# A two-layer decoder trunk: the list of each engine's work is made with the two DMA queues described packet by packet

## The chip, the cores and the metric

One core of one Trainium2 chip. The metric is device time in microseconds (us) of one execution, the median of several. Five engines run their own instruction streams and wait for each other by semaphores: PE (TensorE, matmuls; its weight loads are shown apart as PEld), DVE (VectorE), ACT (ScalarE), POOL (GpSimd) and SP (SyncE, which here only issues transfers). Transfers run in two queues over the same 16 DMA engines: those that SP (and once ACT) issues, called HW below, and those that POOL issues, called SW.

## The reference, cut to what matters

256 tokens of width 1024 in float32 go through two layers, each with a feed-forward part ahead of its attention and one behind it; the feed-forward width is 2816.

```
def swiglu(x, w_in, w_out):
    gate, up = jnp.split(x @ w_in, 2, axis=-1)
    return (jax.nn.silu(gate) * up) @ w_out

for layer in range(DEPTH):                       # DEPTH = 2
    h = h + 0.5 * swiglu(rms_norm(h, ffn1_norm[layer]), ffn1_w_in[layer], ffn1_w_out[layer])
    hn = rms_norm(h, mix_norm[layer])
    if layer < 1:
        q, k, v = heads(hn @ sb_w_qkv[layer])
        h = h + stick_breaking_attention(q, k, v) @ sb_w_o[layer]
    else:
        q = rotary(hn @ swa_w_q[0])
        h = h + sliding_window_sink_attention(q, k_shared, v_shared, sinks) @ swa_w_o[0]
    h = h + 0.5 * swiglu(rms_norm(h, ffn2_norm[layer]), ffn2_w_in[layer], ffn2_w_out[layer])
    if layer == 0:
        k_shared, v_shared = split(rms_norm(h, kv_norm) @ kv_w)
return rms_norm(h, final_norm)
```

## The kernel before, in words

**Stages.** The program runs, one after the other, FFN1 of layer 0 (the first feed-forward stage), stick-breaking attention, FFN2 of layer 0 (the second), the shared keys and values with FFN1 of layer 1 (the third), sliding-window attention, FFN2 of layer 1 (the fourth), and the last norm.

**Numbers.** A float32 product is made of three matmuls of 512 columns (one *step*): weights and activations are each split in a high part and the rest, and hi·hi, hi·lo and lo·hi are added up in PSUM. So each weight tile (1 MB, `raw`) is loaded by SP (`dma`, L369), cast on ACT to `w_hi` (L419), and DVE subtracts to get `w_lo` (L421), each in two halves of 1024 columns. All matmuls of weights have line L288.

**A feed-forward stage.** The first product (gate and up) is done in column blocks. Most blocks use a scheme with seven products in place of eight (`strassen`). Its four weight tiles r11, r12, r22 and r21 are loaded on SP. DVE forms r11 += r12 and later r11 += r22 (L611, two halves each). Two more sums are not made by DVE but by a *fetch* (L616): POOL issues a transfer that adds a block of weights from memory onto the tile, once onto r12 and once onto r11. Each fetch must wait until the earlier content of its tile has been cast, that is for a certain half of `w_lo` on DVE; the product with the tile follows when the fetch has landed and ACT and DVE have cast it. The last product of each stage's first part is the one on the r11 of the last block, after its second fetch. Meanwhile PE does the second product (the *out* weights, `w_out`, two rows of 128 a tile) of earlier blocks, its steps with `aT_h` and `aT_l` as moving operands.

There are five `raw` buffers. A load is issued on SP when the buffer's earlier content has been cast, so that a `w_lo` on DVE also releases SP's next load. `aT_l` (L498), `p`, `u`, `s`, `m` (L786, L789) are DVE's other work: the lower parts of transposed activations and the gating.

**What sets the order.** The code does not issue instructions directly. It makes tasks (`T`), each with an engine, a planned duration, what it reads and writes, and a priority. `Plan.order` lists them: `listed` simulates the five engines as servers that take, among their ready tasks, the one of highest priority; `due` goes back from the end and gives each task of the other engines the time at which PE must have it; with these as new priorities it lists again, four times, and the list with the shortest planned end is emitted. So durations in the plan decide the order of instructions on each engine. In the plan of before a load is a task on SP that lasts its bytes over a fixed rate, and the next load begins when it ends; 2000 ns more pass until its readers may start. A fetch is a task of 1500 on POOL and, in the same row on SP, an empty one that lasts its bytes over 170 (`ADDING`). Loads and fetches thus stand in one row, one at a time.

Of the kernel before, what the change touches and what calls it, by code (L numbers as in the profile page):

```python
# [17 lines left out]
P = 128  # L18
# [62 lines left out]
HEAD = 700.0  # L81
PASSES = 4
# [5 lines left out]
class Task:  # L88
    __slots__ = ("eng", "dur", "fn", "prio", "deps", "outs", "left", "ready", "start", "end", "seq", "lat")

    def __init__(self, eng, dur, fn, prio, seq, lat):
        self.lat = lat
# [23 lines left out]
class Plan:  # L116
# [3 lines left out]
    def add(self, eng, dur, fn, r=(), w=(), prio=None, lat=None):  # L120
# [19 lines left out]
        t.deps.discard(t)  # L140
        self.tasks.append(t)
        return t

    def lag(self, t, o):
        return t.lat if t.lat is not None else 0.0 if o.eng == t.eng and t.eng != "SP" else LAT[t.eng]

    def listed(self, prio):
        free = {e: HEAD for e in LAT}
        wait = {e: [] for e in LAT}
        queue = {e: [] for e in LAT}  # L150
        for t in self.tasks:
            t.ready, t.left = 0.0, len(t.deps)
            if t.left == 0:
                heapq.heappush(wait[t.eng], (t.ready, t.seq, t))
        done = []
        while True:
            best = None
            for e in LAT:
                if queue[e]:
                    at = free[e]  # L160
                elif wait[e]:
                    at = max(free[e], wait[e][0][0])
                else:
                    continue
                if best is None or at < best[0]:
                    best = (at, e)
            if best is None:
                break
            at, e = best
            while wait[e] and wait[e][0][0] <= at:  # L170
                t = heapq.heappop(wait[e])[2]
                heapq.heappush(queue[e], (prio[t.seq], t.seq, t))
            t = heapq.heappop(queue[e])[2]
            t.start = at
            free[e] = at + t.dur
            t.end = at + t.dur
            done.append(t)
            for o in t.outs:
                o.ready = max(o.ready, t.end + self.lag(t, o))
                o.left -= 1  # L180
                if o.left == 0:
                    heapq.heappush(wait[o.eng], (o.ready, o.seq, o))
        assert len(done) == len(self.tasks)
        return done, max(t.end for t in done)

    def due(self, done):
# [5 lines left out]
        for t in sorted(done, key=lambda t: (-t.start, -t.seq)):  # L192
            due[t.seq] = min([last.get(t.seq, 1e18)] + [due[o.seq] - self.lag(t, o) - t.dur for o in t.outs])
# [34 lines left out]
def kernel(  # L228
# [139 lines left out]
    def dma(src, dst, nbytes, w, prio, r=()):  # L368
        T("SP", nbytes / (283.0 if prio < -8.5e5 + 50 else 375.0 if prio < -8e5 else PLAIN), lambda: nc.sync.dma_start(out=dst(), in_=src), r=r, w=w, prio=prio)  # L369
# [245 lines left out]
    def fetch(dst, src):  # L615
        T("POOL", 1500, lambda: nc.gpsimd.dma_start(out=dst.ap, in_=src, accum_op=ALU.add), w=[(dst, 0), (dst, 1)],  # L616
          prio=plan.pos - LOADS, lat=500.0)
        T("SP", P * 2048 * 4 / ADDING, lambda: None, w=[(dst, 0), (dst, 1)], prio=plan.pos - LOADS)
# [895 lines left out]
    def last(t, pair):  # L1514
# [44 lines left out]
        for j, c, ks in ((0, slice(0, 320), (0,)), (1, cuts[1], (640,)), (0, slice(320, 640), (0, 512))):  # L1559
# [8 lines left out]
            T(by, 500, lambda j=j, c=c, now=now, q=nc.scalar if by == "ACT" else nc.sync: q.dma_start(out=out[0, ts(t), c], in_=hg[j].ap[:, now]),  # L1568
              r=[(hg[j], ("to", c.start))], prio=1e9)
# [42 lines left out]
```

## Time and profile before

| | |
|---|---|
| median of three runs | 923.02 us (922.31 to 923.92) |
| the profiled execution | 924.5 us, of it the profile's span 922.7 us |
| mean granted clock of PE | 0.997 |
| matmuls | 4420 |
| bytes moved | 214.43 MB, mean 232 GB/s |

How to read it: a group's line has the source line, the engine, the operation, what it writes and reads, a count, its busy time, the mean in ns, and the idle time just before with what ended it. In the waits, "PEld ps L288 <- DVE w_lo L421" means that the weight load of a matmul waited for DVE's w_lo; total, number and longest follow. In a timeline, a row has the start, the length, the instruction with its count, and in brackets the idle time ahead of it. In the table by stretches each engine's busy time is followed by its count, and the three numbers at the end are the granted clock of PE (1.00 is full), the DMA engines' busy share and GB/s. In the DMA view the last number is the time from issue to landing.

### The profile page before, as it was taken

Reading aid. Unit: us, or ns where it says so; the run is one execution under the profiler, and the core shown is the slowest. Engines: PE = TensorE matmul, PEld = TensorE weight load, DVE = VectorE, ACT = ScalarE, POOL = GpSimd, SP = SyncE. Lnnn points to the kernel's source line nnn. Section 1 sums busy time; section 2 is a strip of 40 time slices with the busy share of each in tenths; the row PEclk is TensorE's granted clock in tenths of the full one; section 3 lists DMA queues with packets and bytes.
Section 4 is the critical chain, followed back from the end, with each engine's and each line's share of the span. In section 5 each row is a group of like instructions: output and inputs, shape, how many; then the busy total and the mean of one; then the engine's idle time right before and its main releaser. Section 6 shows DMA issues by size and latency. Waiting matters only on the chain.

```text
span 922.7 us, 11848 instructions
## 1 busy us (share of the span) xinstructions
PE 905.2 (98%) x4420; PEld 739.5 (80%) x4420; DVE 816.6 (89%) x989; ACT 646.3 (70%) x935; POOL 66.8 (7%) x71
## 2 busy tenths in 40 slices
PE   9999999999999999999999999999999999999997
PEld 6888888788888877778788887887897787787776
DVE  8989898787967999898889999987789799999887
ACT  7867566777987865685588667755868676668563
POOL 2001010000000101010001001100000010001000
PEclk9999999999999999999999999999999999999999
DMA  9897999896752699989795999999843269998981
GB/s 336 302 255 191 299 300 244 260 267 190 242 183 92 138 272 273 242 261 258 206 337 156 246 255 260 288 280 244 305 151 115 92 146 259 303 230 250 302 220 46
DMA packets 107305, 214.43 MB, mean 232 GB/s; under 512 B 6256, under 2 KB 27760, under 8 KB 107248
## 3 DMA queue, kind: packets, MB, share of 16 engines
q1 hardware_dynamic: 85184, 170.49, 52.7%
q0 software_dynamic: 21648, 42.99, 27.1%
q8 instruction: 34, 0.56, 0.2%
q10 hardware_dynamic: 416, 0.20, 0.1%
q14 instruction: 23, 0.19, 0.1%
HBM read 212.62 MB, written 1.05 MB: 232 GB/s over the span
## 4 chain that ended last, share of the span: by engine, by line
PE 41%; DVE 24%; DMA 19%; issue 10%; ACT 6%; POOL 0%; ACTq 0%; POOLq 0%; DVEq 0%; SPq 0%
PE ps L288 38%; DMA raw<-in_ffn_w_in_dram 18%; DVE w_lo L421 15%; ACT w_hi L419 5%; DVE raw L611 4%; PE ps L491 1%; DVE aT_l L498 1%; PE ps L677 1%; PE ps L1346 1%; DMA raw<-in_ffn_w_out_dram 1%; DVE s L587 0%; DVE S_l L581 0%; DVE u L786 0%; DVE xT L498 0%; DVE p L786 0%
## 5 line engine op out<-in xcount | busy, mean ns | idle before, releaser
L421 DVE TENSOR_TENSOR w_lo<-raw,w_hi 128x1024 fp32r<-128x1024 f32 x424 | 498.3, 1217 | 52.9 <-ACT w_hi L419 51.7
L419 ACT CAST w_hi<-raw 128x1024 fp32r<-128x1024 f32 x424 | 424.4, 1050 | 141.5 <-DMA raw<-in_ffn_w_in_dram 69.8
L288 PE MATMUL ps<-w_hi,xT 128*128 128x512 f32 (+1 forms) x788 | 231.6, 378 | 1.9 <-ACT w_hi L419 1.8
L288 PEld LDWEIGHTS ps<-w_hi,xT 128*128 128x128 f32 x788 | 143.0, 190 | 28.9 <-ACT w_hi L419 2.9
L288 PE MATMUL ps<-w_lo,xT 128*128 128x512 f32 (+1 forms) x394 | 148.4, 377 | 2.1 <-DVE w_lo L421 2.0
L288 PE MATMUL ps<-w_hi,aT_h 128*128 128x512 f32 x354 | 140.0, 396 | 0.0
L288 PE MATMUL ps<-w_lo,aT_h 128*128 128x512 f32 x354 | 137.7, 389 | 0.0
L288 PE MATMUL ps<-w_hi,aT_l 128*128 128x512 f32 x354 | 137.4, 388 | 0.0
L288 PE MATMUL ps<-w_lo,S_h 128*128 128x512 f32 x320 | 126.1, 394 | 1.4 <-DVE w_lo L421 1.3
L288 PE MATMUL ps<-w_hi,S_h 128*128 128x512 f32 x320 | 126.2, 394 | 0.1
L288 PE MATMUL ps<-w_hi,S_l 128*128 128x512 f32 x320 | 124.7, 390 | 0.0
L611 DVE TENSOR_TENSOR raw<-raw 128x1024 f32<-128x1024 f32 x78 | 93.7, 1218 | 1.0 <-DMA raw<-in_ffn_w_in_dram 0.8
L288 PEld LDWEIGHTS ps<-w_lo,xT 128*128 128x128 f32 x394 | 74.5, 189 | 18.4 <-DVE w_lo L421 5.1
L616 POOL DMA_DIRECT2D raw<-in_ffn_w_in_dram x38 | 48.1, 1266 | 517.6 <-ACT w_hi L419 209.2
L288 PEld LDWEIGHTS ps<-w_lo,aT_h 128*128 128x128 f32 x354 | 66.5, 188 | 14.1
L288 PEld LDWEIGHTS ps<-w_hi,aT_l 128*128 128x128 f32 x354 | 66.6, 188 | 12.9
L288 PEld LDWEIGHTS ps<-w_hi,aT_h 128*128 128x128 f32 x354 | 66.5, 188 | 12.8
L288 PEld LDWEIGHTS ps<-w_lo,S_h 128*128 128x128 f32 x320 | 60.0, 188 | 18.6 <-DVE w_lo L421 6.2
L288 PEld LDWEIGHTS ps<-w_hi,S_h 128*128 128x128 f32 x320 | 60.1, 188 | 12.2 <-ACT u L782 0.5
L288 PEld LDWEIGHTS ps<-w_hi,S_l 128*128 128x128 f32 x320 | 60.1, 188 | 12.1
L497 ACT CAST aT_h<-ps 128x512 fp32r<-128x512 f32 (+1 forms) x48 | 26.3, 547 | 56.1 <-PE ps L677 56.1
L288 PE MATMUL ps<-xT,w_hi 128*128 128x512 f32 (+1 forms) x136 | 47.0, 395 | 0.0
(184 smaller groups left out, 942.3 us busy)
## 6 DMA issues: line engine op xcount, KB each, us to landing
raw<-in_ffn_w_in_dram SPq DMA_DIRECT2D x76, 1024.0 KB, 8.7
raw<-in_ffn_w_out_dram SPq DMA_DIRECT2D x44, 1024.0 KB, 6.4
raw<-in_ffn_w_in_dram POOLq DMA_DIRECT2D x38, 1024.0 KB, 9.3
raw<-in_sb_w_qkv_dram SPq DMA_DIRECT2D x12, 1024.0 KB, 8.8
raw<-in_ffn_w_in_dram SPq DMA_DIRECT2D x16, 512.0 KB, 6.6
raw<-in_ffn_w_in_dram SPq DMA_DIRECT2D x16, 256.0 KB, 5.5
raw<-in_sb_w_o_dram SPq DMA_DIRECT2D x4, 1024.0 KB, 5.7
raw<-in_swa_w_q_dram SPq DMA_DIRECT2D x4, 1024.0 KB, 9.1
```

The lines of the kernel that those rows point to most:

```text
L288: PE.matmul(ps, lhsT=lhsT, rhs=rhs, start=start, stop=stop, skip_group_check=True)
L419: T("ACT", act(m), lambda sl=sl: ACT.copy(out=flat(hi)[:, sl], in_=flat(raw)[:, sl]), r=[(raw, i) for i in rs] + first, w=[(hi, i) for i i ...
L421: T("DVE", dve(m), lambda sl=sl: DVE.tensor_sub(out=flat(lo)[:, sl], in0=flat(raw)[:, sl], in1=flat(hi)[:, sl].bitcast(F32)), r=[(raw, i) ...
L491: PE.matmul(bank.ap[:, i * P:(i + 1) * P], lhsT=s, rhs=ident, start=i == 0, stop=True, is_transpose=True, skip_group_check=True)
L497: T("ACT", act(n), lambda: ACT.copy(out=hi[2](), in_=src()), r=B(bank), w=[hi[0:2]])
L498: T("DVE", dve(n), lambda: DVE.tensor_sub(out=lo[2](), in0=src(), in1=hi[2]().bitcast(F32)), r=B(bank) + [hi[0:2]], w=[lo[0:2]])
L611: T("DVE", dve(m), lambda sl=sl: DVE.tensor_add(out=flat(dst)[:, sl], in0=flat(dst)[:, sl], in1=flat(src)[:, sl]), r=[(src, k) for k in ks ...
L616: T("POOL", 1500, lambda: nc.gpsimd.dma_start(out=dst.ap, in_=src, accum_op=ALU.add), w=[(dst, 0), (dst, 1)], prio=plan.pos - LOADS, lat=5 ...
L677: PE.transpose(out=tr.ap[:, i * P:(i + 1) * P], in_=m.ap[:, i * P:(i + 1) * P], identity=ident)
L1346: PE.matmul(z[par].ap[:, i_ * P:(i_ + 1) * P], lhsT=e.ap[:, par * 384 + c:par * 384 + c + P], rhs=ident, start=i_ == 0, stop=True, is_tran ...
```

## The change

`Plan.listed` becomes a simulation by events. A task may carry `moves`: a queue (HW or SW), a number of packets for each DMA engine and the ns of one. Issuing costs its engine 500 (SP) or 1000 (POOL); after a set-up time the transfer joins its queue; the two queues' heads share the DMA engines in turn, a packet of each; after the last packet and a landing time the task has ended. `due` takes a task's whole time from start to end. Nothing else of the program is edited: the tasks, what they read and write and their given priorities stay, and so does the work on every engine.

```
+RAMP = 500.0
+SETUP = {"HW": 1200.0, "SW": 1700.0}
+LANDS = {"HW": 900.0, "SW": 500.0}
+ISSUE = 500.0
+PACKET = {4096: 157.0, 2048: 84.0, 1024: 50.0}
+ADDED = 176.0
...
     def lag(self, t, o):
-        return t.lat if t.lat is not None else 0.0 if o.eng == t.eng and t.eng != "SP" else LAT[t.eng]
+        return 0.0 if t.moves else t.lat if t.lat is not None else 0.0 if o.eng == t.eng else LAT[t.eng]
...
+        def begin(e, now):
+            if ready[e] and free[e] <= now:
+                t = heapq.heappop(ready[e])[2]
+                t.start = now
+                free[e] = now + t.dur
+                done.append(t)
+                at(free[e], "free", t)
+                if t.moves:
+                    at(now + SETUP[t.moves[0]], "moves", t)
+                else:
+                    at(free[e], "end", t)
...
+        while events or queues["HW"] or queues["SW"]:
+            heads = {k: q[0] for k, q in queues.items() if q}
+            total = sum(h[2] for h in heads.values())
+            next_ = [(last + h[1] * total / h[2], k) for k, h in heads.items()]
+            over = min(next_) if next_ else (1e18, None)
+            now = min(over[0], events[0][0] if events else 1e18)
+            for h in heads.values():
+                h[1] -= (now - last) * h[2] / total
+            last = now
+            if over[0] <= now:
+                t = queues[over[1]].popleft()[0]
+                at(now + LANDS[over[1]], "end", t)
+                continue
+            while events and events[0][0] <= now:
+                _, _, what, t = heapq.heappop(events)
+                if what == "moves":
+                    k, n, each = t.moves
+                    queues[k].append([t, n * each + (0.0 if heads else RAMP), each])
+                elif what == "end":
+                    ended(t, now)
+                elif what == "ready":
+                    heapq.heappush(ready[t.eng], (prio[t.seq], t.seq, t))
             for e in LAT:
...
-            due[t.seq] = min([last.get(t.seq, 1e18)] + [due[o.seq] - self.lag(t, o) - t.dur for o in t.outs])
+            due[t.seq] = min([last.get(t.seq, 1e18)] + [due[o.seq] - self.lag(t, o) - (t.end - t.start) for o in t.outs])
...
     def dma(src, dst, nbytes, w, prio, r=()):
-        T("SP", nbytes / (283.0 if prio < -8.5e5 + 50 else 375.0 if prio < -8e5 else PLAIN), lambda: nc.sync.dma_start(out=dst(), in_=src), r=r, w=w, prio=prio)
+        size = max(p for p in PACKET if p == 1024 or p <= 4 * src.shape[-1])
+        T("SP", ISSUE, lambda: nc.sync.dma_start(out=dst(), in_=src), r=r, w=w, prio=prio, moves=("HW", nbytes / size / 16, PACKET[size]))
...
     def fetch(dst, src):
-        T("POOL", 1500, lambda: nc.gpsimd.dma_start(out=dst.ap, in_=src, accum_op=ALU.add), w=[(dst, 0), (dst, 1)],
-          prio=plan.pos - LOADS, lat=500.0)
-        T("SP", P * 2048 * 4 / ADDING, lambda: None, w=[(dst, 0), (dst, 1)], prio=plan.pos - LOADS)
+        T("POOL", 1000, lambda: nc.gpsimd.dma_start(out=dst.ap, in_=src, accum_op=ALU.add), w=[(dst, 0), (dst, 1)],
+          prio=plan.pos - LOADS, moves=("SW", P * 2048 * 4 / 2048 / 16, ADDED))
```

The source lines behind the edit move down by 28 to 30: w_lo is L421 before and L451 after, the sum L611 and L641, the fetch L616 and L646, SP's loads L369 and L399, the matmul L288 and L317.

Three places show what becomes of the order. Numbers behind a name count buffers and are not the same before and after. The first is DVE near the end of the third feed-forward stage, around the `w_lo` that releases the stage's last fetch. Before, raw_4872 is r11, onto which the fetch adds, and raw_4936 is the tile of the other product:

```order
L611 TENSOR_TENSOR raw_4872<-raw_4872,raw_4936 128x1024
L421 TENSOR_TENSOR w_lo_5008<-raw_4872,w_hi_4996 128x1024
L421 TENSOR_TENSOR w_lo_5017<-raw_4936,w_hi_4981 128x1024
L421 TENSOR_TENSOR w_lo_5008<-raw_4872,w_hi_4996 128x1024
L421 TENSOR_TENSOR w_lo_5017<-raw_4936,w_hi_4981 128x1024
L421 TENSOR_TENSOR w_lo_5044<-raw_4962,w_hi_5022 128x1024 x2
L421 TENSOR_TENSOR w_lo_5059<-raw_4894,w_hi_5049 128x1024 x2
```

and of the change, where raw_4803 is r11, raw_4841 the other tile, and raw_4909 the out weights' tile (raw_4962 before):

```order
L451 TENSOR_TENSOR w_lo_4990<-raw_4803,w_hi_4958 128x1024 x2
L451 TENSOR_TENSOR w_lo_5013<-raw_4841,w_hi_4971 128x1024 x2
L451 TENSOR_TENSOR w_lo_5029<-raw_4825,w_hi_5006 128x1024 x2
L451 TENSOR_TENSOR w_lo_5051<-raw_4909,w_hi_5036 128x1024
L528 TENSOR_TENSOR aT_l_4883<-ps_66,aT_h_4876 128x4x128
L451 TENSOR_TENSOR w_lo_5051<-raw_4909,w_hi_5036 128x1024
```

Before, the two products' halves alternate, so that r11 is free after the third `w_lo` and the other tile after the fourth; in the change r11 is free after the second and the other tile two later, and the r12 product's `w_lo` (raw_4825) come ahead of the out weights'.

The second place is PE a little later, at the stage's last product. Before, its weights are w_hi_5118 and w_lo_5128; w_hi_5022 and w_hi_5140 are out weights:

```order
L288 MATMUL ps_66<-w_hi_5022,aT_h_4867 128x512
L288 MATMUL ps_66<-w_hi_5022,aT_l_4878 128x512
L288 MATMUL ps_66<-w_lo_5044,aT_h_4867 128x512
L288 MATMUL ps_66<-w_hi_5118,xT_163 128x512 x2
L288 MATMUL ps_66<-w_lo_5128,xT_163 128x512
...
L288 MATMUL ps_66<-w_hi_5140,aT_h_5113 128x512
L288 MATMUL ps_66<-w_hi_5140,aT_l_5120 128x512
L288 MATMUL ps_66<-w_lo_5149,aT_h_5113 128x512
```

and of the change, where they are w_hi_5121 and w_lo_5134, and w_hi_5103 is the out weight of raw_5034, whose `w_lo` DVE has ahead of the last product's:

```order
L317 MATMUL ps_66<-w_hi_5103,aT_h_5108 128x512
L317 MATMUL ps_66<-w_hi_5103,aT_l_5119 128x512
L317 MATMUL ps_66<-w_lo_5113,aT_h_5108 128x512
L317 MATMUL ps_66<-w_hi_5121,xT_176 128x512 x2
L317 MATMUL ps_66<-w_lo_5134,xT_176 128x512
...
L317 MATMUL ps_66<-w_hi_5103,aT_h_5108 128x512
L317 MATMUL ps_66<-w_hi_5103,aT_l_5119 128x512
L317 MATMUL ps_66<-w_lo_5113,aT_h_5108 128x512
```

Steps of the out weights that stood ahead of the last product stand behind it: two here, six in the second stage, three in the fourth, one in the first.

The third place is SP at the program's start, before:

```order
L369 DMA hN_63<-in_x_dram 128x512 x2
L369 DMA raw_113<-in_ffn1_w_in_dram 128x512 x4
L369 DMA hN_63<-in_x_dram 128x512 x2
L369 DMA raw_185<-in_ffn1_w_in_dram 128x512 x4
L369 DMA raw_214<-in_ffn1_w_in_dram 128x512 x4
```

and of the change:

```order
L399 DMA hN_63<-in_x_dram 128x512 x2
L399 DMA raw_100<-in_ffn1_w_in_dram 128x512 x2
L399 DMA hN_63<-in_x_dram 128x512
L399 DMA raw_100<-in_ffn1_w_in_dram 128x512
L399 DMA hN_63<-in_x_dram 128x512
L399 DMA raw_100<-in_ffn1_w_in_dram 128x512
```

The second half of x (two tiles of `hN`) goes between the four parts of the first weight tile instead of behind them.

More of the change, by code (lines that the diff above doesn't have):

```diff
@@ L81 @@
 HEAD = 700.0
+RAMP = 500.0
[4 more added lines that the diff above has]
+ADDED = 176.0
 PASSES = 4
 class Task:
-    __slots__ = ("eng", "dur", "fn", "prio", "deps", "outs", "left", "ready", "start", "end", "seq", "lat")
+    __slots__ = ("eng", "dur", "fn", "prio", "deps", "outs", "left", "ready", "start", "end", "seq", "lat", "moves")
     def __init__(self, eng, dur, fn, prio, seq, lat):
-        self.lat = lat
+        self.lat, self.moves = lat, None
         self.eng, self.dur, self.fn, self.prio, self.seq = eng, dur, fn, prio, seq
@@ L118, in __init__, with add @@
         self.tasks, self.pos = [], 0.0
-    def add(self, eng, dur, fn, r=(), w=(), prio=None, lat=None):
+    def add(self, eng, dur, fn, r=(), w=(), prio=None, lat=None, moves=None):
         t = Task(eng, dur, fn, self.pos if prio is None else prio, len(self.tasks), lat)
@@ L140, in add @@
         t.deps.discard(t)
+        t.moves = moves
         self.tasks.append(t)
@@ L144, in lag, with at, ended @@
     def lag(self, t, o):
-        return t.lat if t.lat is not None else 0.0 if o.eng == t.eng and t.eng != "SP" else LAT[t.eng]
+        return 0.0 if t.moves else t.lat if t.lat is not None else 0.0 if o.eng == t.eng else LAT[t.eng]
     def listed(self, prio):
         free = {e: HEAD for e in LAT}
-        wait = {e: [] for e in LAT}
-        queue = {e: [] for e in LAT}
+        ready = {e: [] for e in LAT}
+        events, made = [], [0]
+        queues, last, done = {"HW": deque(), "SW": deque()}, 0.0, []
+        def at(time, what, t):
+            made[0] += 1
+            heapq.heappush(events, (time, made[0], what, t))
+        def begin(e, now):
[9 more added lines that the diff above has]
+                    at(free[e], "end", t)
+        def ended(t, now):
+            t.end = now
+            for o in t.outs:
+                o.ready = max(o.ready, now + self.lag(t, o))
+                o.left -= 1
+                if o.left == 0:
+                    at(max(o.ready, HEAD), "ready", o)
         for t in self.tasks:
@@ L153, in listed @@
             if t.left == 0:
[L154 to L157, printed above, removed]
-            for e in LAT:
[L159 to L182, printed above, removed]
+                at(HEAD, "ready", t)
+        while events or queues["HW"] or queues["SW"]:
[20 more added lines that the diff above has]
+                    heapq.heappush(ready[t.eng], (prio[t.seq], t.seq, t))
+            for e in LAT:
+                begin(e, now)
         assert len(done) == len(self.tasks)
@@ L1567, in last @@
             by = "ACT" if t == j == 1 else "SP"
-            T(by, 500, lambda j=j, c=c, now=now, q=nc.scalar if by == "ACT" else nc.sync: q.dma_start(out=out[0, ts(t), c], in_=hg[j].ap[:, now]),
-              r=[(hg[j], ("to", c.start))], prio=1e9)
+            T(by, ISSUE, lambda j=j, c=c, now=now, q=nc.scalar if by == "ACT" else nc.sync: q.dma_start(out=out[0, ts(t), c], in_=hg[j].ap[:, now]),
+              r=[(hg[j], ("to", c.start))], prio=1e9, moves=("HW", 8, PACKET[1024]))
     ffn(ffn2_w_in[1], ffn2_w_out[1], (A0, (4, 3) if NEWACC else A1), ((2, 5) if NEWACC else A2) + A3, last, ending=True, blocks=BL[3], roots=roots4)
```

## The prediction

> **What bounds the kernel now.** First the page: busy shares, then the costliest groups.
>
> ```profile
> PE 905.2 (98%) x4420; PEld 739.5 (80%) x4420; DVE 816.6 (89%) x989; ACT 646.3 (70%) x935; POOL 66.8 (7%) x71
> L421 DVE TENSOR_TENSOR w_lo<-raw,w_hi 128x1024 fp32r<-128x1024 f32 x424 | 498.3, 1217 | 52.9 <-ACT w_hi L419 51.7
> ```
>
> TensorE is occupied all but through, and the change leaves it the same 4420 matmuls. So the whole prize is time in which PE waits or runs slowly. The waits of the weight loads, which show the waits that the pipelined matmuls hide, are these four lines:
>
> ```profile
> PEld ps L288 <- DVE w_lo L421: 11.3, 19, 1.0
> PEld ps L677 <- DVE m L789: 4.8, 5, 1.5
> PEld ps L288 <- ACT w_hi L419: 3.6, 5, 1.7
> PEld ps L677 <- DVE aT_l L498: 3.2, 7, 0.8
> ```
>
> Together 22.9 us. That, and what a slowed clock costs, is the most that any order of the same work can win. The largest single place is the end of the third feed-forward stage (FFN1 of layer 1), in the timeline of PE and in the table by stretches:
>
> ```profile
> 643.64 0.39 PE L288 MATMUL ps<-w_hi,aT_l 128*128 128x512 f32 x1
> 643.86 0.39 PE L288 MATMUL ps<-w_lo,aT_h 128*128 128x512 f32 x1
> 645.50 0.73 PE L288 MATMUL ps<-w_hi,xT 128*128 128x512 f32 x2 [1.25 <-ACT w_hi L419]
> 646.76 0.77 PE L288 MATMUL ps<-w_lo,xT 128*128 128x512 f32 x1 [0.53 <-DVE w_lo L421]
> 647.33 1.06 PE L288 MATMUL ps<-w_hi,xT 128*128 128x512 f32 x2
> ...
> 645.10:650.00 4.90, 3.98 (x10) 2.90 (x11) 4.52 (x4) 3.18 (x4) 0.00 (x0) 0.67 0.16 45
> ```
>
> Normal pace is 643.86 − 643.64 = 0.22 us, call it 0.227, a matmul. After idle times of 1.25 and 0.53 us two matmuls take 1.06 − 0.39 + 0.23 ≈ 0.86 us instead of 0.45 (the granted clock is 0.67 in the stretch). Some eight or nine matmuls at 0.2 us extra make 1.8 us, so the place costs 1.25 + 0.53 + 1.8 and small change, 3.9 us. The Trainium skill (TensorE: Matmul & The Clock Gate, "Part 1: The HAM clock gate (the "warmup" mystery)") has the clock halved only after an idle window of about 3.4 us; by that rule there would be no 1.8 us here. The row goes against it, and the row decides: a stall under 2 us can cost as much again.
>
> What PE waits for there is the last fetch (an accumulating transfer of 1 MB that POOL issues), then the cast on ACT, then w_lo on DVE. The chain that ended last shows the last fetch of each of the four stages, and what follows one of them:
>
> ```profile
> 147.41 12.89 DMA raw<-in_ffn_w_in_dram
> ...
> 442.67 12.99 DMA raw<-in_ffn_w_in_dram
> ...
> 455.68 1.06 ACT w_hi L419
> ...
> 456.76 1.24 DVE w_lo L421
> ...
> 597.80 12.70 DMA raw<-in_ffn_w_in_dram
> 629.93 14.44 DMA raw<-in_ffn_w_in_dram
> ...
> 883.59 13.83 DMA raw<-in_ffn_w_in_dram
> ```
>
> Fetches are not always that long. These are two others, from the DMA view of 505 to 516 us and of 566 to 578 us:
>
> ```profile
> raw<-in_ffn_w_in_dram POOLq DMA_DIRECT2D x1, 1024.0 KB, 8.7
> ...
> raw<-in_ffn_w_in_dram POOLq DMA_DIRECT2D x1, 1024.0 KB, 10.2
> ```
>
> And this is when POOL issued them, beside the next load that SP issued:
>
> ```profile
> 505.74 1.27 POOL L616 DMA_DIRECT2D raw<-in_ffn_w_in_dram  x1 [10.58 <-DVE w_lo L421]
> ...
> 566.52 1.27 POOL L616 DMA_DIRECT2D raw<-in_ffn_w_in_dram  x1 [8.48 <-DVE w_lo L421]
> ...
> 509.64 8.17 SPq L369 DMA_DIRECT2D raw<-in_ffn_w_in_dram  x3
> ...
> 568.47 9.71 SPq L369 DMA_DIRECT2D raw<-in_ffn_w_in_dram  x4
> ...
> 598.64 9.67 SPq L369 DMA_DIRECT2D raw<-in_ffn_w_in_dram  x4
> ...
> 630.78 4.87 SPq L369 DMA_DIRECT2D raw<-in_ffn_w_out_dram  x2
> ```
>
> With the next load 3.9 us after the fetch (509.64 − 505.74) it takes 8.7 us, with 1.95 us 10.2, with 0.84 us 12.7, with 0.85 us 14.4. **How soon a plain load follows a fetch sets the fetch's length**; on this reading the forecast rests.
>
> **The change, part by part.** No work is added or taken away: both orders hold the same matmuls, casts, sums and transfers, so the busy times are priced at no change. What moves is the order, and the sum is of waits. It is made against the profiled execution (924.5 us, span 922.7); the median shown is 1.5 us less, and I carry the difference over to it.
>
> *End of the third stage.* In DVE's rows before (shown with the change) the two products' w_lo alternate: the third frees the tile that the fetch writes, the fourth, one w_lo later, frees the tile that SP's next load writes. Here is that run of w_lo, and DVE at the end of the fetch:
>
> ```profile
> 626.09 9.16 DVE L421 TENSOR_TENSOR w_lo<-raw,w_hi 128x1024 fp32r<-128x1024 f32 x8
> ...
> 645.48 3.50 DVE L421 TENSOR_TENSOR w_lo<-raw,w_hi 128x1024 fp32r<-128x1024 f32 x3 [3.31 <-ACT w_hi L419]
> ```
>
> Eight in 9.16 us are 1.14 each. In the changed order the two w_lo of the first product stand together: the fetch is released one w_lo, 1.14 us, earlier, and the load after two w_lo, 2.3 us behind it, instead of one. By the four distances above the fetch should then take about 10.2 rather than 14.4 us (11 to 12 if the load after that, another 2.3 us on, also counts). It lands 1.1 + 2.4 to 4.2 = 3.5 to 5.3 us earlier. PE comes to the product earlier too, by one step pair: six matmuls, 6 × 0.227 = 1.36 us, stand behind it now (PE's rows). And ACT and DVE have an out weight's casts ahead of the fetched tile's: two w_lo, 2.3 us, in a stretch where DVE idled 3.31. Its load is issued 2.3 us after the fetch and lands about when the fetch does; that can hold the fetched tile up by 1 to 2 us. Needed: 1.25 + 0.53 + 1.36 = 3.1 us. Taken: **−3.0** of the 3.9, half a wait left without a slow clock; from −3.9 to +0.2 (fetch as long as before: 1.36 − 1.14).
>
> *End of the fourth stage.* The same rewriting of DVE's order, and nine matmuls (2.04 us) moved behind the product. The fetch lands 1.1 + 3.6 (13.83 to 10.2) = 4.7 us earlier at best. What can be won at the end is small, and inside the stage PE waits for sums and triggers:
>
> ```profile
> 899.80 0.50 PE L288 MATMUL ps<-w_lo,xT 128*128 128x512 f32 x1 [0.53 <-DVE w_lo L421]
> ...
> PE ps L677 <- DVE m L789: 1.8, 2, 1.1
> ```
>
> The first line is the end, the second from the waits of 760 to 900 us. Between the first and the last fetch DVE has the same count of w_lo and sums, but one less ahead of the last. I take 0.5 at the end and half of the 1.8: **−1.4**; from −4 to +0.9 (2.04 − 1.14, fetch as before).
>
> *Second stage (FFN2 of layer 0).* Here the loop fetch, casts, sums, next fetch is tight throughout, and the end waits too:
>
> ```profile
> 456.78 0.73 PE L288 MATMUL ps<-w_hi,xT 128*128 128x512 f32 x2 [0.51 <-ACT w_hi L419]
> 458.04 0.50 PE L288 MATMUL ps<-w_lo,xT 128*128 128x512 f32 x1 [0.53 <-DVE w_lo L421]
> ...
> 300.39 1.30 POOL L616 DMA_DIRECT2D raw<-in_ffn_w_in_dram  x1 [7.61 <-ACT xT L497]
> 301.21 2.08 POOL L523 TENSOR_TENSOR small<-small,mhalf 128x1 f32<-128x1 f32 x1
> ```
>
> Counting DVE's list from the release of the first fetch to that of the last: 95 operations of 1.14 us before, 92 now, and some 2 us of short ones less: 5.4 us earlier. One fetch gains its two-w_lo distance (−3.5 us), one loses it (+2), and the first waits for a second power on POOL that now stands ahead of it (+1 of the 2.08). At the end the out weights' loads follow the last fetch at 1.1, 3.4 and 5.7 us instead of 0.8 and 5.9, some +1.5. Sum: the last product's weights 4.4 us earlier. But six steps, 18 matmuls or 4.08 us, have moved behind that product, so if the fetch sets the end, little is left: −0.3. If PE sets it, all its waits of the stage go, 6 us. Taken nearer to the fetch: **−1.0**; from −6 to +1.8 (4.08 less two w_lo).
>
> *First stage.* PE hardly waits there. One fetch loses its clear distance (next load at 1.1 us after it rather than 4.9; 9.3 becomes about 13), the last one is released two w_lo earlier, with more loads close behind it, and one step (0.68 us) moves behind the last product. **+0.8**; from −0.7 to +2.5.
>
> *Start.* SP's first rows (shown with the change) send the tiles of x for the second half ahead of two weight tiles.
>
> ```profile
> 5.95 3.60 PE L288 MATMUL ps<-raw,x_f 128*128 128x512 f32 x8
> 9.38 0.63 PE L491 MATMUL ps<-ident,hN 128*128 128x128 f32 x4
> ...
> 1.65 1.85 SPq L369 DMA_DIRECT2D raw<-in_ffn_w_in_dram  x4
> 3.54 0.91 SPq L369 DMA_DIRECT2D hN<-in_x_dram  x2
> ```
>
> Eight matmuls in 3.60 us is half the normal pace, paced by what arrives. SP issues one tile per 0.46 us (1.85/4); two weight tiles come one and two places later, 0.5 to 0.9 us, and the transposes at 9.38, which now have their data earlier, win some of it back. **+0.6**, from 0 to 0.9. The two attention stages get small moves both ways: 0, ±1.
>
> Sum: −3.0 − 1.4 − 1.0 + 0.8 + 0.6 = **−4.0 us**: 920.5 for a profiled execution, 919.0 for the median.
>
> **The rivals.** *Slower.* A fetch is as long as the bytes of plain loads beside it make it, however they are spaced; the 10.2 us would be an accident of what was on the way. For it: 12.7 and 14.4 us at the same distance of 0.85, so distance is not all. Against it: 8.7 and 10.2 us with three and four loads issued within 9.7 us. Then the last fetches gain only their earlier release, 2.27, 2.27, 1.14 and 1.14 us, against steps moved behind of 0.68, 4.08, 1.36 and 2.04: 0 (a wait of 0.7 at most to win), +1.8, +0.2, +0.9, with first stage and start +1.4: +4.3, and 1.8 more if the longer wait at 452 us slows the clock as at 645. That is 927.3, or 929 with the spell, and 925 to 926 if the shorter lists of the second stage help. It decides at the second stage: if its last fetch lands less than 4.1 us earlier, measured against PE's order. The Trainium skill (DMA: Bandwidth & Descriptors, "Queues, rings and completion order") has each DMA engine take packets from its queues in turn; by that rule alone this rival is right, since a fetch shares with whatever is queued. The 8.7 us beside three loads speak against it as the whole story.
>
> *No change.* The distances won (three fetches inside the stages and the ends of the third and fourth) and lost (three inside) cancel, PE being 98% busy anyway: within 1.8 us, 923.
>
> *More.* Fetches land before PE wherever the loop got shorter, and most of the 6 us of the second stage and 3.9 of the third go, with 2 to 3 of the fourth: −12 and +1 at start, about 912.
>
> **How the numbers follow.** Forecast (−2 to −8): 0.50. More: 0.09. No change: 0.19. Slower: 0.22. A measurement of this kernel can tell about 0.2%, 1.85 us, from no change; so faster 0.59, same 0.19, slower 0.22. The range from 911 to 926.5 takes in most of the larger gain and about half of the slower case (925 to 929). The forecast's own range is 915 to 921.
>
> **What would show it.** Right: POOL's last fetch of the third stage about 10 to 12 us long, the half-speed matmuls behind it gone, granted clock 1.00 there; the next load 2.3 us behind the fetch in SP's rows. The fourth stage's last fetch equally short. At the second stage's end a wait of PE of 0 to 3 us for w_hi and w_lo. At the start the eight direct matmuls stretched beyond 3.60 us. Wrong: last fetches still over 13 us; a new wait of PE on an out weight's w_lo ahead of the last product; a slow stretch behind the second stage's end; waits of PE inside the first stage, where there were none.

## The result, and the profile after

The changed kernel takes 934.93 us (median of 4 runs, 934.16 to 936.2), beside 923.47 us before (922.31 to 924.49): a ratio of 1.0126, 95% interval 1.0108 to 1.0144. It is slower by 1.3%, where a gain of 4 us was forecast. The profiled execution has a span of 932.4 us, 9.7 more than before.

The first lines of the page of the changed kernel:

```profile
PE 907.6 (97%) x4420; PEld 744.0 (80%) x4420; DVE 818.8 (88%) x989; ACT 647.0 (69%) x935; POOL 63.5 (7%) x71
L451 DVE TENSOR_TENSOR w_lo<-raw,w_hi 128x1024 fp32r<-128x1024 f32 x424 | 498.7, 1218 | 42.6 <-ACT w_hi L449 41.8
```

The work is the same: 4420 matmuls, and busy times within 4.5 us on every engine. So the 9.7 us are waiting and slow clock. The table by stretches tells where (engines in the order PE, PEld, DVE, ACT, POOL). Before:

```profile
300.00:460.00 160.00, 157.23 (x697) 125.47 (x696) 145.04 (x151) 106.07 (x131) 14.38 (x11) 1.00 0.86 237
460.00:652.00 192.00, 189.69 (x857) 155.27 (x856) 176.99 (x196) 135.46 (x181) 13.88 (x12) 0.99 0.88 254
760.00:900.00 140.00, 136.66 (x610) 109.92 (x609) 127.72 (x129) 91.33 (x109) 10.20 (x8) 1.00 0.92 259
```

and after:

```profile
300.00:460.00 160.00, 153.79 (x676) 124.46 (x675) 146.52 (x151) 107.34 (x132) 13.31 (x11) 0.98 0.88 246
460.00:652.00 192.00, 188.93 (x856) 154.99 (x855) 175.24 (x194) 134.18 (x179) 13.87 (x12) 0.99 0.85 247
760.00:900.00 140.00, 135.37 (x601) 109.89 (x600) 131.42 (x131) 93.20 (x112) 11.47 (x9) 0.99 0.91 257
```

In the second feed-forward stage PE does 21 matmuls fewer in the same 160 us: 21 × 0.227 = 4.8 us behind. In the third it holds its place, in the fourth it loses another nine. Comparing when the same number of matmuls has begun in both timelines says it finer. PE is behind by 0.1 us when the second stage begins, by 1.7 just ahead of that stage's last product (at 450 us) and by 4.7 behind it; by 7.8 at 640 us, inside the third stage, and by 4.7 again behind its end; by 5.7 when the fourth begins, 9.2 at 880 us, and 9.7 at the end. So the insides of the three stages cost 1.6, 3.1 and 3.5 us, the end of the second another 3.0, and only the end of the third wins, 3.1.

What PE waits for is a line that was small before (2.6 us in 4 waits). The waits of the changed kernel, in total us, number and longest:

```profile
PE ps L706 <- DVE m L818: 9.0, 6, 2.4
PE ps L317 <- ACT w_hi L449: 2.3, 1, 2.3
PE ps L317 <- DVE w_lo L451: 2.0, 4, 0.7
```

`m` is the gate: silu times up, the result of a block, which PE transposes next. The worst place, in PE's timeline, with the row of the table around it:

```profile
402.27 0.50 PE L317 MATMUL ps<-w_lo,S_h 128*128 128x512 f32 x1 [0.65 <-DVE w_lo L451]
405.21 0.99 PE L706 MATMUL ps<-ident,m 128*128 128x128 f32 x4 [2.43 <-DVE m L818]
405.85 0.77 PE L317 MATMUL ps<-w_hi,S_h 128*128 128x512 f32 x1
406.42 0.63 PE L317 MATMUL ps<-w_hi,S_l 128*128 128x512 f32 x1
...
402.00:409.00 7.00, 4.29 (x13) 3.35 (x14) 7.00 (x8) 6.10 (x9) 0.00 (x0) 0.76 1.07 255
```

0.65 and 2.43 us of waiting, then matmuls at 0.63 in place of 0.39: the clock is down to 0.76 over the stretch. DVE is busy for all of its 7.00 us. Its own timeline shows how it came to be late; first before, where the gate comes after nine operations:

```profile
392.50 4.63 DVE L421 TENSOR_TENSOR w_lo<-raw,w_hi 128x1024 fp32r<-128x1024 f32 x4 [4.12 <-ACT w_hi L419]
397.05 2.35 DVE L611 TENSOR_TENSOR raw<-raw 128x1024 f32<-128x1024 f32 x2
399.45 3.50 DVE L421 TENSOR_TENSOR w_lo<-raw,w_hi 128x1024 fp32r<-128x1024 f32 x3
402.86 0.74 DVE L789 SCALAR_TENSOR_TENSOR m<-p,small,m 128x512 f32<-128x512 f32 x1
```

and after, where eleven stand ahead of it (three, then sums and w_lo in turn, then three):

```profile
391.54 3.50 DVE L451 TENSOR_TENSOR w_lo<-raw,w_hi 128x1024 fp32r<-128x1024 f32 x3 [4.64 <-ACT w_hi L449]
395.07 1.23 DVE L641 TENSOR_TENSOR raw<-raw 128x1024 f32<-128x1024 f32 x1
...
399.86 1.23 DVE L641 TENSOR_TENSOR raw<-raw 128x1024 f32<-128x1024 f32 x1
401.00 3.49 DVE L451 TENSOR_TENSOR w_lo<-raw,w_hi 128x1024 fp32r<-128x1024 f32 x3
404.41 0.75 DVE L818 SCALAR_TENSOR_TENSOR m<-p,small,m 128x512 f32<-128x512 f32 x1
```

Both wait over 4 us for the fetched tile (through ACT's cast of it); then the list runs without a gap. The same holds at most block ends of the second to fourth stage: between the fetched tile's first w_lo and the gate 6 to 9 operations stood before (8 here), 9 to 14 stand now, mostly 10.

The ends of the stages came out as follows: third stage (650.97, 652.31), second (456.63, 457.89).

```profile
650.97 0.61 PE L317 MATMUL ps<-w_hi,xT 128*128 128x512 f32 x2
652.31 0.50 PE L317 MATMUL ps<-w_lo,xT 128*128 128x512 f32 x1 [0.72 <-DVE w_lo L451]
...
456.63 1.22 PE L317 MATMUL ps<-w_hi,xT 128*128 128x512 f32 x2 [2.29 <-ACT w_hi L449]
457.89 0.80 PE L317 MATMUL ps<-w_lo,xT 128*128 128x512 f32 x1
```

At the third stage's end the wait and the half-speed matmuls are gone but for 0.72 us, as forecast. At the second's PE now waits 2.29 us and goes on slowly. The last fetches of the two stages, in the DMA view, third stage first:

```profile
raw<-in_ffn_w_in_dram POOLq DMA_DIRECT2D x1, 1024.0 KB, 11.5
...
raw<-in_ffn_w_in_dram POOLq DMA_DIRECT2D x1, 1024.0 KB, 15.4
```

The first took 14.4 us before, the second 13.0.

### The profile page after: what moved, and what is told of

The parts are those of the page before. It is cut to its first block, busy times and chain, and to the rows that moved or that the text cites. A ratio compares the mean times of both kernels' runs of the same rounds, so it can differ in the third digit from the quotient of the medians.

```text
span 932.4 us, 11864 instructions
## 1 busy us (share of the span) xinstructions
PE 907.6 (97%) x4420; PEld 744.0 (80%) x4420; DVE 818.8 (88%) x989; ACT 647.0 (69%) x935; POOL 63.5 (7%) x71
## 4 chain that ended last, share of the span: by engine, by line
PE 35%; DVE 30%; DMA 19%; issue 12%; ACT 4%; POOL 0%; POOLq 0%; ACTq 0%; DVEq 0%; SPq 0%
PE ps L317 33%; DVE w_lo L451 19%; DMA raw<-in_ffn_w_in_dram 17%; DVE raw L641 5%; ACT w_hi L449 3%; DMA raw<-in_ffn_w_out_dram 2%; PE ps L521 1%; DVE aT_l L528 1%; DVE s L617 1%; DVE m L818 1%; DVE S_l L611 1%; DVE e L1367 0%; DVE u L815 0%; PE ps L1375 0%; PE ps L706 0%
## 5 line engine op out<-in xcount | busy, mean ns | idle before, releaser
L451 DVE TENSOR_TENSOR w_lo<-raw,w_hi 128x1024 fp32r<-128x1024 f32 x424 | 498.7, 1218 | 42.6 <-ACT w_hi L449 41.8
L317 PE MATMUL ps<-w_hi,xT 128*128 128x512 f32 (+1 forms) x788 | 234.0, 381 | 2.6 <-ACT w_hi L449 2.3
L317 PEld LDWEIGHTS ps<-w_hi,xT 128*128 128x128 f32 x788 | 145.1, 192 | 30.1 <-ACT w_hi L449 2.7
L317 PE MATMUL ps<-w_lo,xT 128*128 128x512 f32 (+1 forms) x394 | 148.7, 377 | 1.1 <-DVE w_lo L451 1.1
L317 PE MATMUL ps<-w_hi,aT_h 128*128 128x512 f32 x354 | 140.3, 396 | 0.6 <-ACT aT_h L527 0.6
L317 PE MATMUL ps<-w_hi,aT_l 128*128 128x512 f32 x354 | 137.5, 388 | 0.9 <-DVE aT_l L528 0.9
L317 PE MATMUL ps<-w_lo,aT_h 128*128 128x512 f32 x354 | 137.7, 389 | 0.0
L317 PE MATMUL ps<-w_lo,S_h 128*128 128x512 f32 x320 | 126.0, 394 | 1.3 <-DVE w_lo L451 1.0
L317 PE MATMUL ps<-w_hi,S_h 128*128 128x512 f32 x320 | 126.6, 396 | 0.0
L317 PE MATMUL ps<-w_hi,S_l 128*128 128x512 f32 x320 | 125.2, 391 | 0.4 <-DVE S_l L611 0.4
L641 DVE TENSOR_TENSOR raw<-raw 128x1024 f32<-128x1024 f32 x78 | 94.8, 1221 | 2.6 <-DMA raw<-in_ffn_w_in_dram 1.4
L317 PEld LDWEIGHTS ps<-w_lo,xT 128*128 128x128 f32 x394 | 75.1, 191 | 16.2 <-DVE w_lo L451 2.7
L646 POOL DMA_DIRECT2D raw<-in_ffn_w_in_dram x38 | 48.1, 1265 | 507.9 <-DVE raw L641 194.1
L317 PEld LDWEIGHTS ps<-w_hi,aT_l 128*128 128x128 f32 x354 | 66.6, 188 | 14.1 <-DVE aT_l L528 1.2
L317 PEld LDWEIGHTS ps<-w_lo,aT_h 128*128 128x128 f32 x354 | 66.5, 188 | 14.2
L317 PEld LDWEIGHTS ps<-w_hi,aT_h 128*128 128x128 f32 x354 | 66.5, 188 | 13.6 <-ACT aT_h L527 1.0
L317 PEld LDWEIGHTS ps<-w_lo,S_h 128*128 128x128 f32 x320 | 60.3, 189 | 16.0 <-DVE w_lo L451 3.4
L317 PEld LDWEIGHTS ps<-w_hi,S_l 128*128 128x128 f32 x320 | 60.4, 189 | 12.7 <-DVE S_l L611 0.8
L317 PEld LDWEIGHTS ps<-w_hi,S_h 128*128 128x128 f32 x320 | 60.2, 188 | 12.0 <-ACT u L811 0.2
L317 PE MATMUL ps<-xT,w_hi 128*128 128x512 f32 (+1 forms) x136 | 47.0, 395 | 0.0
```

Source lines behind the costliest of these rows:

```text
L317: PE.matmul(ps, lhsT=lhsT, rhs=rhs, start=start, stop=stop, skip_group_check=True)
L451: T("DVE", dve(m), lambda sl=sl: DVE.tensor_sub(out=flat(lo)[:, sl], in0=flat(raw)[:, sl], in1=flat(hi)[:, sl].bitcast(F32)), r=[(raw, i) ...
L641: T("DVE", dve(m), lambda sl=sl: DVE.tensor_add(out=flat(dst)[:, sl], in0=flat(dst)[:, sl], in1=flat(src)[:, sl]), r=[(src, k) for k in ks ...
L646: T("POOL", 1000, lambda: nc.gpsimd.dma_start(out=dst.ap, in_=src, accum_op=ALU.add), w=[(dst, 0), (dst, 1)], prio=plan.pos - LOADS, moves ...
```

## The experiments

The kernel before has medians of 923.47 to 925.99 us on the chips used, so each run is compared with runs of the kernel before on its own chip; the ratio has its 95% interval, and runs on different chips are compared by their ratios. The edits that move single instructions use a list added to the planner: a task's number, and how many places earlier (or, below zero, later) it stands on its engine; the emitted list is then put in an order in which every task still follows all that it depends on.

```
+EARLIER = {1561: 2, 1562: 2, ...}
...
+        for seq, n in EARLIER.items():
+            row = engines[self.tasks[seq].eng]
+            i = row.index(self.tasks[seq])
+            row.insert(i - n, row.pop(i))
```

### The gate two places earlier, and two places later

`m_back` moves silu on ACT and the gate on DVE two places earlier in the changed order at six block ends, `m_late` two places later in the order of before.

```
+EARLIER = {1561: 2, 1562: 2, 1668: 2, 1669: 2, 2255: 2, 2256: 2, 2362: 2, 2363: 2, 3235: 2, 3236: 2, 3342: 2, 3343: 2}
```

> The order of the change, except that at six block ends the gate m (the product of silu and up whose transposes PE waits for) stands two places earlier on ACT (silu) and two places earlier on DVE. Theory A, the gate was put too late: the waits of PE for m at 402, 437, 597, 631, 849 and 884 us, with the half-speed stretches behind them 16.6 us in all, shrink to about the 4 to 6 us that the order of before has at these places; 934.9 becomes 923 to 927. Theory B, the loop of fetches is what PE waits for, and m only shows it: the casts that now come later on DVE release the fetches later and PE waits for w_lo in place of m; 933 to 936.

> The order of before, except that at the same six block ends the gate m stands two places later on ACT and on DVE. Theory A: new waits of PE for m of 1 to 3 us each at 403, 435, 593, 623, 845 and 876 us, some with a half-speed stretch behind them; 923.5 becomes 929 to 936. Theory B: PE has other reasons to wait in the changed order; here at most 0.5 us a place, 923 to 926.

Measured: m_back 935.82 us, ratio to before 1.0108 (1.0087 to 1.0129), not told apart from the change (1.0126, 1.0108 to 1.0144) and within the 933 to 936 of theory B. The waits for m did go, and others took their place. The waits of m_back and, at the place shown above, its timeline:

```profile
PE ps L343 <- ACT ps L867: 7.2, 6, 1.7
PE ps L343 <- ACT w_hi L475: 2.8, 1, 2.8
...
403.03 0.66 PE L732 MATMUL ps<-ident,m 128*128 128x128 f32 x4 [0.16 <-DVE m L844]
...
405.71 0.74 PE L343 MATMUL ps<-w_hi,xT 128*128 128x512 f32 x2 [1.32 <-ACT ps L867]
```

m's wait is 0.16 in place of 2.43, and three matmuls later PE waits 1.32 for the next thing from ACT. So theory A falls in its simple form: the gate is the first to be late, not the only one. Theory B named the w_lo as what PE would wait for instead; it was mostly ACT's work (7.2 us in 6 waits). m_late took 926.41, 1.0014 (0.9999 to 1.003): far less than theory A's 929 to 936, though with waits far longer than theory B's 0.5 us. Its waits for m grew from 2.6 to 7.2 us (2.60 us at 406, 3.45 at 847), but with PE held there, its waits at the stage ends shrank. A wait that is put in ahead of a fetch's product covers one behind it.

### Whole pieces of one engine's order exchanged

`six_back` puts 18 instructions each of ACT and DVE at the six block boundaries back in the order of before, within the changed order; `six_in` does the opposite; `pe_back` gives the changed order the PE rows of before in three stages.

```
+GIVEN = ((1553, 1555, 1570, ...), (1554, 1556, 1571, ...), ...)
...
+        for row in GIVEN:
+            here = engines[self.tasks[row[0]].eng]
+            these = set(row)
+            given = iter(row)
+            engines[self.tasks[row[0]].eng][:] = [self.tasks[next(given)] if t.seq in these else t for t in here]
```

> The order of the change, except that at six block boundaries (of the blocks at 390, 424, 585, 618, 838 and 871 us) 18 instructions each of ACT and of DVE, from the fetched tile's casts to the release of the next block's last fetch, stand in the order of before. Theory C, the change puts the sums and the casts that feed the next fetch ahead of those that PE needs next, and DVE and ACT have no time to spare there: the waits of PE at 402, 437, 597, 631, 849 and 884 us with their half-speed stretches, 16.6 us, shrink to 4 to 7; 934.9 becomes 924 to 927. Theory D, the loss hangs on PE's order or on when tiles land, not on this order: 932 to 936.

> The order of before, with the same six pieces of ACT's and DVE's order taken from the change. Theory C: the six waits appear, 923.5 becomes 930 to 936. Theory D: 922 to 926.

> The order of the change, except that PE's order in the second, third and fourth feed-forward stage is that of before. Theory D (PE reaches gates and products earlier because steps were moved behind them): the waits inside the stages go, 934.9 becomes 924 to 929. Theory C: the waits inside the stages stay, only the end of the second stage (2.45 us and its slow stretch) gains; 931 to 934, and the third stage's end waits as long as in the changed order or less.

All three expectations failed, two of them by far. six_back took 949.08 us, 1.0255 (1.0235 to 1.0275); pe_back 958.82, 1.0365 (1.034 to 1.0389). An engine's order can't be judged without those of the others: PE's order of before has transposes at places where the changed DVE order has not yet come to the operation that they wait for. The largest waits, of six_back and of pe_back:

```profile
PE ps L362 <- ACT w_hi L494: 13.5, 8, 4.6
...
PE ps L742 <- DVE aT_l L564: 15.2, 5, 5.8
```

six_in took 928.89, 1.0043 (1.0023 to 1.0064), within neither expectation. PE's waits for m came up from 2.6 to 8.8 us, with 2.43 us at 407 as in the change at 405, so this piece of ACT's and DVE's order, beside a fetch as long as before (13.8 us at 378, 13.7 before), is enough for that wait. But it also brought the short last fetches of the third and fourth stage (10.9 and 10.4 us) with it, which pay back part. No single engine's order explains the loss by these runs. The next ones change the lengths of the fetches.

### The end of the second stage

`end2` puts three of the six steps that had moved behind the last product ahead of it again.

```
+EARLIER = {1779: 4, 1780: 4, 1781: 4}
```

> The order of the change, except that at the end of the second stage three out-weight steps (nine matmuls, 2.04 us) that the change had put behind the last product stand ahead of it again on PE. Theory: the wait for the fetched tile at 454 us, 2.45 and 0.44 us, falls by 2.04, and the half-speed stretch behind it (some 1.4 us) goes; 934.9 becomes 931 to 933. Rival: the order of PE there is worth nothing since the stretch after it is set by ACT and DVE; 934 to 936.

934.22 us, 1.0099 (1.0074 to 1.0125). By the times that is 0.7 us less than the change, by the ratios some 2.5, and the two intervals overlap, so the time doesn't decide. In the traces PE is 1.3 us better off behind the stage's end. At the last product it waits 0.43 and 0.52 us, and the clock stays full, as the theory has it; but it then waits 1.27 us for the m behind it, as the rival has it: DVE's work after the fetch takes back a part.

### The fetches' length alone

`apart` takes the order of before and puts the two w_lo of one product together ahead of four fetches, as the change has it, so that SP's next load follows the fetch at 2.0 us and not at 0.8. `apart2` does so at the last fetch of the third and fourth stage only, `apart3` at that of the second too.

```
+EARLIER = {1405: 1, 2109: 1, 2436: 1, 3426: 1}   # apart
+EARLIER = {2436: 1, 3426: 1}                     # apart2
+EARLIER = {1732: 1, 2436: 1, 3426: 1}            # apart3
```

> The order of before, except that at four places (fetches at 346.6, 537.2, 629.9 and 883.6 us) the two w_lo of the fetched tile's earlier content stand together on DVE, so that the fetch is released one w_lo earlier and SP's next load 2.3 us behind it in place of 1.1. Theory of the prediction: these four fetches take 9 to 12 us in place of 13.1 to 14.4, the wait and the half-speed stretch of 3.9 us at 644 us go, and the time falls by 3 to 6 us, to 917.5 to 920.5. Rival: the fetches get shorter but PE is held by the gates and casts in between; 922 to 924.

> The order of before, except that the two w_lo ahead of the last fetch of the third and the fourth stage stand together (fetches at 629.9 and 883.6 us; the other two places of the run apart are left as before, since a new wait of 2.8 us came at one of them). Theory of the prediction's first term: both fetches take 9 to 12 us, PE's waits at 644 (3.9 us with the slow stretch) and at 899 us go, 924.0 becomes 919 to 921. Rival: as in apart, what is won is given back in waits for w_lo of the other product of the pair; 922 to 924.

> The run apart2 (order of before, the two w_lo together ahead of the last fetch of the third and fourth stage) with the same edit at the last fetch of the second stage too (442.7 us, 13.0 us long). That fetch takes 10 to 11 us and the wait of 1.0 us at 457 us goes: 0.5 to 1.5 us below apart2, that is 0.992 to 0.994 of before. Rival: a new wait for the other product's w_lo ahead of it; 0.994 to 0.997.

apart took 922.93, 0.9987 (0.997 to 1.0004), the time of the rival. In its trace, of the slowest of ten executions (926.77), the four fetches took 9.5, 9.9, 10.5 and 10.9 us in place of 13.1 to 14.4, and the 3.9 us at 644 went; but at the first place PE reached the other product, whose w_lo was now a place later:

```profile
349.13 0.39 PE L314 MATMUL ps<-w_hi,S_l 128*128 128x512 f32 x1
352.17 0.50 PE L314 MATMUL ps<-w_lo,S_h 128*128 128x512 f32 x1 [2.65 <-DVE w_lo L447]
```

Without that place, apart2 took 920.42, 0.9943 (0.9925 to 0.9961), and its span is 918.7, 4.0 less than before, most of what the two ends had cost (3.9 and 1.0 us). So the first term of the prediction is shown by itself, with one reserve that holds for all exchanges of this kind: the fetch also starts one w_lo earlier, so that not all of the gain need be its length. apart3 took 920.23, 0.9959 (0.9943 to 0.9974). Its fetch took 10.3 us and the wait at 457 us went, as expected; but the time can't be told from that of apart2 and lies in the rival's range, not in the 0.992 to 0.994 that was expected, although no new wait of PE shows there.

The opposite place is the changed order itself. `after_apart` puts the w_lo together ahead of its six inner fetches whose next load follows at 0.8 us, and touches nothing else:

```
+EARLIER = {1498: 1, 1605: 1, 2192: 1, 2299: 1, 3172: 1, 3279: 1}
```

> The order of the change, except that ahead of the six fetches inside the stages whose next load follows at 0.8 us (376, 410, 571, 604, 824 and 857 us) the two w_lo of the tile stand together, so that the load follows at 2 us. Theory E: these fetches take 9 to 11 us in place of 12.9 to 14.2, land as the plan has them, and the waits for m at 402, 437, 597, 631, 849 and 884 us (16.6 us with the slow stretches) fall to under 5; 934.9 becomes 922 to 927. Theory C: the fetches get shorter and the waits stay; 931 to 936.

916.80 us, 0.9923 (0.9908 to 0.9938): six exchanges of two neighbours on DVE take 2.0%, some 18 us, off the changed kernel. The fetch that PE's worst wait hung on, in the DMA view of the changed kernel and of after_apart, then POOL's and SP's rows of after_apart:

```profile
raw<-in_ffn_w_in_dram POOLq DMA_DIRECT2D x1, 1024.0 KB, 14.2
...
raw<-in_ffn_w_in_dram POOLq DMA_DIRECT2D x1, 1024.0 KB, 10.7
...
376.88 1.27 POOL L679 DMA_DIRECT2D raw<-in_ffn_w_in_dram  x1 [9.23 <-DVE w_lo L484]
378.85 9.13 SPq L432 DMA_DIRECT2D raw<-in_ffn_w_in_dram  x4
```

SP's load now follows at 378.85 − 376.88 = 1.97 us, and the fetch is 3.5 us shorter. Counted from the fetch before it, it is also released 1.1 us earlier (10.5 us behind that one's issue in place of 11.6), so the tile comes some 4.7 us earlier, three quarters of it by the length. DVE, which had waited 4.64 us for the fetched tile, goes on without a gap, with the same eleven operations ahead of m, and m is there before PE. The table by stretches has the matmuls back:

```profile
300.00:460.00 160.00, 157.98 (x713) 128.68 (x712) 152.45 (x158) 111.72 (x139) 13.31 (x11) 1.00 0.91 256
760.00:900.00 140.00, 138.87 (x625) 113.36 (x626) 133.83 (x139) 92.24 (x112) 10.55 (x9) 1.00 0.87 252
```

Theory E, which expected 922 to 927, named the right cause and undersold it; theory C falls, since the list is otherwise the changed one. The gain reaches the second stage's end too: the last fetch there, left as it was, took 15.9 us but was released at 434.52 in place of 440.07.

### A list made for longer fetches

`sw_late` alters one number of the changed planner and lets it list anew; `sw_late_alt` takes that list and makes its six inner fetches long again.

```
-SETUP = {"HW": 1200.0, "SW": 1700.0}
+SETUP = {"HW": 1200.0, "SW": 3700.0}
```

> The changed planner with one number altered: the set-up of a fetch is 3700 ns in place of 1700, so that a fetch with loads beside it is planned at about 13 us, as the trace of the change shows the inner ones (12.9, 12.9, 13.3, 13.6, 14.2 where the plan has 11.0). Theory E, the list is made for fetches of 11 us and leaves the gate m only 1.3 to 1.8 us of room, so that a fetch 2 to 3 us longer stalls PE at six block ends: with the length right the waits for m of 2 to 2.4 us go; 934.9 becomes 920 to 927. Theory C (sums and casts ahead of the gate are the harm, whatever the fetch's length): the list made so has 11 operations between the fetched tile's w_lo and m, in place of 10, so the waits stay; 933 to 940.

> The order of the run sw_late (914.5), except that ahead of six fetches inside the second, third and fourth stage the two products' w_lo alternate on DVE, so that the next load follows the fetch at 0.8 us in place of 2.0. These fetches become 13 to 14 us long, about what that list was planned for. Theory G, a list planned with the true length bears it: the time rises by at most 4 us, to 914 to 919. Theory F, short fetches are the whole gain, and any list loses as the changed one did when they are long: the waits for m come back at several block ends, 923 to 935.

sw_late took 914.45 us, 0.9899 (0.9885 to 0.9914), the fastest of all, faster than both kernels of this change and than the 920 to 927 of theory E. Theory C falls once more: with eleven operations between the fetched tile's first w_lo and m at the six places, where the changed order has nine or ten, hardly any wait for m is left:

```profile
PE ps L706 <- DVE m L818: 1.2, 2, 0.8
```

Its list has two properties at once: fetches planned as long as they are when disturbed, and, from the second stage on, no load closer than 1.7 us behind a fetch, so that in its trace the inner fetches take 8.5 to 12.1 us. sw_late_alt tells the two apart: with 12.8 to 14.3 us at the six places it took 925.43, 0.9999 (0.9989 to 1.0009). By the ratios that is 1.0% more than sw_late, near theory F, but 1.3% less than the changed kernel with fetches as long, and no slower than the kernel before. Waits for m come to 3.2 us in 6, none over 0.7:

```profile
PE ps L739 <- DVE m L851: 3.2, 6, 0.7
```

So both count. Short fetches, with their earlier release, are worth 1.0% in this list and 2.0% in the changed one, and a list planned with the longer fetch bears long ones better.

## Why the prediction was wrong, point by point

- **What bounds the kernel** was right: PE's waits and the slow clock behind them are the whole difference.
- **How soon a load follows a fetch sets its length** was right in the main. In 14 profiles of this study together, 123 feed-forward fetches whose next load follows within 1 us took 13.3 us (median, 10.3 to 15.9); 70 at 1.5 to 2.3 us took 10.5 (9.0 to 15.3); 160 at 4 to 6 us took 8.6 (8.2 to 11.8). The ranges overlap, so the distance isn't all. DVE was busy for 98% to 100% of the first 2.5 us behind the issue in all three groups, so its work doesn't part them. (In the working for the half-speed matmuls, 1.06 − 0.39 + 0.23 is 0.90 and not 0.86; nothing hangs on it.)
- **End of the third stage**, −3.0: right, in size and mechanism. The last fetch fell from 14.4 to 11.5 us, its next load came 1.9 us behind it, and PE's loss there fell from 3.9 to 1.0. But PE's waits inside this stage were priced at nothing, and cost 3.1 us.
- **Fourth stage's end**, a gain of 0.5: wrong in sign. The fetch fell only to 12.5 us, and the aT_h that PE needs had come to stand on ACT behind the cast of an out weight whose load landed at 902.1:

```profile
903.76 0.50 PE L317 MATMUL ps<-w_hi,aT_h 128*128 128x512 f32 x1 [0.58 <-ACT aT_h L527]
905.13 0.50 PE L317 MATMUL ps<-w_hi,aT_l 128*128 128x512 f32 x1 [0.88 <-DVE aT_l L528]
```

- **Second stage**, −1.0 (measured +4.6, outside its bounds of −6 to +1.8), and the insides of the third and fourth: this is the step that failed, in two parts.
  - *Inside the stages.* The prediction counted DVE's operations from the release of one fetch to that of the next and took that as the whole price of DVE's order. The count held: from the first release to the last it gave 5.4 us less, with the lost and won distances 6.9, and measured were 5.8. What PE needs from DVE between the two, the gate m first, was not counted; its waits were taken to shrink and grew from 2.6 to 9.0 us. The gate stands 9 to 14 operations behind the fetched tile in place of 6 to 9, in a list that, by the planner's own times, leaves it 1.3 to 1.8 us of room if the fetch takes 11.0 us. With 12.9 to 14.2 us the room is used up, PE waits about 2 us, and three of these waits cost nearly as much again at half speed. That the place alone is not the cause is shown by m_back (no gain) and sw_late (eleven between, and hardly a wait); that on this list the late landing of the tiles is, by after_apart (2.0% less).
  - *At the second stage's end*, where 3.0 of the 4.6 us were lost, the last product's weights were to come 4.4 us earlier. The fetch landed at 455.51 in place of 455.66 us, 0.15 earlier, while 4.08 us of steps had moved behind the product. The first fetch of the stage was issued 3.2 us later and not 1, and the last took 15.4 us in place of 13.0, 2.4 longer and not 1.5.
- The same error sits in **the fetches lost and won inside the stages**, which were set off against each other at 2 to 3.5 us each. Their number is unchanged, six of 12.7 us or more inside before and after, but the runs show a price that depends on the list: 1.0% for six of them in that of sw_late, 2.0% in the changed one.
- **The first stage and the start**, +0.8 and +0.6: not settled. The trace shown is behind by 0.3 to 0.5 us at 33 to 66 us, and by 0.1 when the second stage begins; but the other traces with the same order up to there (m_back, end2, six_back, pe_back, after_apart) are behind by 0.3 to 1.7 then, and those with the order of before by 0.4 to 0.8, once by 4.4. The fetch that lost its distance took 10.3 us, not the 13 that were priced.
- **The slower rival** ended on the right side (+4 to +6, where 11.5 were measured). Its mechanism, last fetches no shorter than before, was seen in the first and second stage (12.9 us became 13.8, 13.0 became 15.4); in the third and fourth they did get shorter.
- The rule for the clock in the Trainium skill (TensorE: Matmul & The Clock Gate, "Part 1: The HAM clock gate (the "warmup" mystery)"), an idle window of about 3.4 us, is again not what the traces show: waits of 0.65 and 2.43 us were followed by a clock of 0.76. The length of the window does show, but it need not be idle throughout (last section).

Left open: why the two plans differ so in how much a long fetch costs. That sw_late_alt bears them 1.3% better is shown; which of its differences does it was not tried. Nor was a fetch made shorter without an earlier release, which would part the two.

## What to carry to other kernels

When a scheduler's model changes, check for every wait on a transfer how long the trace says it takes in that very neighbourhood, and how much room the list leaves behind it; count to the next thing the busy engine needs, not only to the next transfer. Two instructions exchanged on an engine that is not the bound can put 1.1 us more between a transfer and the load behind it, and make the transfer 3.5 us shorter. A wait removed at one place may only uncover the next, and orders of single engines taken from two good lists can make a bad one.

## What the runs showed of the hardware that was not expected

- A 1 MB accumulating transfer issued by POOL takes 8.6 us (median) when SP's next load comes 4 to 6 us later and 13.3 when it comes within 1 us, though loads follow within its run in both cases.
- The clock does not fall by the length of the wait alone: waits of 1.25 and 0.53 us (before, 645) and of 2.43 (after, 405) were followed by half-speed matmuls, a wait of 1.70 us at 886 in the changed kernel was not. The clock records of the 14 traces say more. In each, the slow spells start at multiples of 3.41 us from one another, and those inside the program last one such window, at times two. Of the full-speed windows between 20 and 905 us, all 24 in which PE was idle for 1.88 us or more were followed by a slow one, none of the 3549 with less than 1.5, and 3 of the 11 between. So by these traces it counts how much of one such window the waits fill together, and about half is enough. Here are two pairs of windows of the changed kernel:

```profile
401.98:405.39 3.41, 0.68 (x3) 0.37 (x4) 3.41 (x5) 3.41 (x5) 0.00 (x0) 1.00 1.07 190
405.39:408.80 3.41, 3.41 (x11) 2.82 (x11) 3.41 (x4) 2.51 (x4) 0.00 (x0) 0.50 1.07 312
883.26:886.67 3.41, 1.71 (x11) 1.17 (x10) 3.41 (x4) 3.41 (x5) 0.00 (x0) 1.00 1.11 201
886.67:890.08 3.41, 3.41 (x16) 2.80 (x15) 3.41 (x4) 2.05 (x3) 0.68 (x1) 1.00 0.86 246
```

PE was busy for 0.68 us of the first and 1.71 of the third; only the first was followed by half speed.
